# A gate unit at the start and one behind the attention, four scan groups with rows of their own: one change to a hybrid decoder block

## The chip, the cores and the metric

The kernel runs on one core of a Trainium2 chip. The metric is the time of the device for one execution, in microseconds (us). A core has five engines that run side by side, each with an instruction queue of its own, worked off in order: TensorE (PE) for matrix products, VectorE (DVE), ScalarE (ACT), GpSimd (POOL), and SyncE (SP), which here only starts DMA transfers. ACT can start transfers too.

## The reference

One decoder layer over T = 1024 tokens with D = 1024 channels, in float32. Three mixers work on the same normalised input, and sigmoid gates merge them:

```python
h = rms_norm(x, pre_mix_norm)
z, xbc, dt_raw, sb_qkv, nsa_q, nsa_kv, nsa_gate, merge_gate = split(h @ w_in)
y_ssm = ssm_mixer(z, xbc, dt_raw, ...)        # conv, silu, chunked scan in 4 groups, gate by silu(z), norm
y_sb  = stick_breaking_attention(sb_qkv)      # 4 heads of 128, causal, no softmax
y_nsa = nsa_attention(nsa_q, nsa_kv, nsa_gate, ...)  # compressed, selected and window branches, 8 heads of 64
gm = sigmoid(merge_gate).reshape(b, s, 3, D)
mixed = gm[:, :, 0] * (y_ssm @ w_br_ssm) + gm[:, :, 1] * (y_sb @ w_br_sb) + gm[:, :, 2] * (y_nsa @ w_br_nsa)
x = x + rms_norm(mixed @ w_out, post_mix_norm)
h = rms_norm(x, pre_ffn_norm)
gate, val = split(causal_dwconv(h @ ffn_w_up))
return x + rms_norm((gelu(gate) * val) @ ffn_w_down, post_ffn_norm)
```

The scan of a group goes over eight chunks of 128 tokens:

```python
cb = einsum('tn,sn->ts', c, b);  w = cb * decay * dt
y  = einsum('tsh,shp->thp', w, x) + einsum('tn,hpn->thp', c, state) * exp(acum)
state = state * exp(acum[-1]) + einsum('sh,shp,sn->hpn', to_end, x, b)
```

## The kernel before

Channels lie on the partitions and tokens on the free axis. Each float32 operand is split into a rounded part and a rest (`hi`, `lo`; `whi`, `wlo` for weights), and a product is three matmuls: hi·hi, hi·lo, lo·hi. A weight comes by SP's queue into `wraw`; ACT rounds it (`whi`) and POOL subtracts (`wlo`). The order of each engine's instructions is set by a scheduler from the order of the program, the waits between instructions and a model of their durations, so an edit in one place may move instructions in another.

The stages, in order of time in the profiled execution:

- 0 to about 68 us: the input norm in two halves of 512 tokens (`norm`, `normalise`; L440 scales, L442 takes the rest `h_lo`), and small projections with tokens on the partitions (`token_major`; names `ps_t`, `ps_s`, `thi`, `tlo`). Its queries are copied by `q_out` (L434) and stored to memory `q_d` (L435), 16 stores of 128 KB.
- about 65 to 300 us: the scan's inputs (`ssm_units`). Units are computed in pairs by seven products instead of eight. For this, sums of the operand's blocks are made on DVE (`combos`, L537 to L540) and split again by ACT (L561) and DVE (L562); `weights7` prepares the weights' sums. Results go to memory `s_d`: six rows of 128 channels for each of the four groups q (two of x, then B, C, and two of z).
- about 300 to 820 us: sparse attention. While its small steps wait for each other, PE is given pieces of other work: a `Fill` object hands out matmuls of gate units in threes. A gate unit is one block of 128 of the 3072 merge gate channels: 48 matmuls of 128 x 512, a sigmoid in three ACT instructions for each half (L243 to L245, `gate_e`) and two stores to `g_d`. Units 0 to 11 are the fill here (`N_GATES`).
- about 825 to 1171 us: stick-breaking attention, head by head (`sb_stage`). The fill is the next head's projection and gate units 12 to 23 (`SB_GATES` tells which units go with which head, `SB_FILL` how many matmuls per step). In `chain`, a step computes scores (`sa`, `sz`), rounds the running sums (`s_hi` on ACT, `s_lo` on POOL), weights (`w_hi`, `w_lo`) and adds the weighted values into `ps_o` or `ps_b`. Head 3 has no next head: its fill is gate units 18 to 23. At its start, group 0's six rows are loaded.
- about 1168 to 1292 us: the four scans (`ssd_stage`). Each is a generator: in a slot, `front` of a chunk makes `dec` (ACT), `xd` (DVE), `Bc` (ACT) and `W` (POOL), and `back` adds the chunk's result and carries the state. The last slots gate with z, square, and take the mean over channels (one-column matmuls with `ones`), a norm. `SSD_AT` gives the slot in which each group starts. Rows lie in buffers: group 0 in `row` (one buffer each), group 1 in `third`, group 2 in `row` again, group 3 in `row` when group 0 has ended.
- from 1292 us: the branch projections and the merge, the output projection, and the gated MLP with its convolution. `load_y` brings back the mixers' outputs; the last four of its sixteen pieces (k = 12 to 15) use buffers of the scans.

Of the kernel before, what the change touches and what calls it, by code (L numbers as in the profile page):

```python
# [10 lines left out]
F32 = mybir.dt.float32  # L11
R32 = mybir.dt.float32r
# [7 lines left out]
T = 1024  # L20
# [141 lines left out]

N_GATES = 12
SB_GATES = (12, 14, 16, 18, 24)

NSA_FILL = (2, 0)
NSA_SLOTS = 9
# [1 line left out]
NSA_EARLY = 32  # L171
NSA_LEAD = 0
NSA_SWITCH = (10, 1)
SB_FILL = (2.2, 2.2, 2.2, 1.6)

SSD_AT = (0, 2, 9, 12)

X_BUFS = 36

# [16 lines left out]
def trunk(ctx: ExitStack, tc: tile.TileContext, A: dict, outT: bass.AP, dbg=None):  # L196
    nc = tc.nc
# [10 lines left out]
    mm, tr = pe(nc.tensor.matmul), pe(nc.tensor.transpose)  # L208
# [33 lines left out]
    def sigmoid(dst, src):  # L242
        act(dst, src, AF.Exp, scale=-1.0)  # L243
        act(dst, dst, AF.Ln, bias=1.0)
        act(dst, dst, AF.Exp, scale=-1.0)  # L245
# [6 lines left out]
    def scratch(name, shape):  # L252
        scr[name] = dram.tile(shape, F32, name=name, tag=name)
        return scr[name]

    y_d = scratch("y_d", [16 * 128, T])
    g_d = scratch("g_d", [24 * 128, T])
# [38 lines left out]
    def hs(h):  # L296
        return slice(h * 512, (h + 1) * 512)
# [13 lines left out]
    hx = ExitStack()  # L311
# [37 lines left out]
    start = ExitStack()  # L349
# [27 lines left out]
    q_d = scratch("q_d", [2, 8, 128, 256])  # L377
# [4 lines left out]
    xs, tm0 = [[], []], []  # L382
# [49 lines left out]
    def q_out(ci, t, ps, scale):  # L432
        q = tmw.tile([128, 256], F32, name="q_out", bufs=2)
        act(q, ps[:, :256], AF.Copy, scale=scale)  # L434
        nc.sync.dma_start(q_d[ci, t], q)  # L435

    def normalise(h, r):
        for k in range(8):
# [5 lines left out]
    for h, tiles in ((0, [[ps_s, ps_s, ps_t, ps_t]]), (1, [[ps_o, ps_d], [ps_s, ps_s]])):  # L444
        *pss, ss = first_half(h, tiles)
        rq, r = norm(h, ss)
# [15 lines left out]
    U_CMP, U_SB, U_SSM, U_GATE = 0, 2, 14, 38  # L462
# [77 lines left out]
        eng.tensor_tensor(b21, b11, b21, op=OP.add)  # L540


    s_d = scratch("s_d", [24 * 128, T])

    def ssm_units():


        wx = early.enter_context(tc.tile_pool(name="wx0", side="right", reuse_waits="tile", bufs=2))
        ev = early.enter_context(tc.tile_pool(name="ev", side="right", reuse_waits="tile", bufs=2))
        rhs = {q: [None] * 4 for q in range(1, 8)}  # L550
        for k in range(4):
            b = [xs[h][k + n] for n in (0, 4) for h in range(2)]
            combos(*b, V)
            for q, n, h in ((1, 0, 0), (2, 4, 0), (3, 4, 1)):
                rhs[q][k] = h_rhs(k + n, h)
            for q, t in zip((6, 5, 4, 7), b):
                rhs[q][k] = t
        for q in (6, 7, 5, 4):
            for k in range(4):
                t, hi, lo = rhs[q][k], x_t(), x_t()  # L560
                act(hi, t, AF.Copy)  # L561
                V.tensor_tensor(lo, t, fl(hi), op=OP.subtract)  # L562
                rhs[q][k] = hi, lo

        def snap(ps):
            t = x_t(F32)
            act(t, ps, AF.Copy)  # L567
            return t

        for q, m in itertools.product(range(4), (0, 2, 1)):  # L570
            u0 = 6 * q + 2 * m
            halos = [ev.tile([128, 4], F32, name="halo", bufs=4) for _ in range(2)]

            def evict(n, h, ps):
                o = ev.tile([128, 512], F32, name="o")
                if m < 2:
                    cu = q * 4 + 2 * m + n
                    conv(o, h, ps, [pvc(PV_CW, 4 * cu + 3 - d) for d in range(4)], pvc(PV_CB, cu), halos[n])
                act(o, o if m < 2 else ps, AF.Silu)
                nc.sync.dma_start(s_d[(u0 + n) * 128:(u0 + n + 1) * 128, hs(h)], o)  # L580

            w = weights7(wx, A["wfm"][U_SSM + u0], A["wfm"][U_SSM + u0 + 1], 512)
            x, y, z, v = ps_d(), ps_s(), ps_t(), (ps_o, ps_b)[m % 2]()
            product(x, w, rhs, 1, True)
            s1 = snap(x)
            product(y, w, rhs, 2, True)
            V.tensor_tensor(y, y, s1, op=OP.add)
            evict(0, 0, y)
            product(x, w, rhs, 6, False)
            s2 = snap(x)  # L590
            product(z, w, rhs, 7, True)
            product(x, w, rhs, 5, False)
            s3 = snap(x)
            product(v, w, rhs, 4, True)
            V.tensor_tensor(s2, z, s2, op=OP.subtract)
            V.tensor_tensor(v, v, s2, op=OP.add)
            evict(1, 0, v)
            V.tensor_tensor(z, z, s3, op=OP.subtract)
            evict(1, 1, z)
            product(x, w, rhs, 3, False)  # L600
            evict(0, 1, x)
# [2 lines left out]
    tc.keep_in_program_order(nc.scalar.preload_act_table_set(TABLE))  # L604
    early.close()


    gp = hx.enter_context(tc.tile_pool(name="gp", reuse_waits="tile", bufs=2))

    def gates(j0, j1, steps=unit_steps):  # L610
        for j in range(j0, j1):
            def evict(h, ps):
                e = gp.tile([128, 512], F32, name="gate_e")
                sigmoid(e, ps)
                nc.sync.dma_start(g_d[j * 128:(j + 1) * 128, hs(h)], e)
            yield from steps(U_GATE + j, evict)

    both = ExitStack()
    keep = both.enter_context(tc.tile_pool(name="keep", side="right", reuse_waits="tile", bufs=1))
    dte = keep.tile([128, 2, 8, 16], F32, name="dte")  # L620
# [19 lines left out]
    def row_t(n, dt=F32):  # L640
        return hd.tile([128, T], dt, name=f"row{n}")

    def ssm_rows(q, row=row_t):
        rows = [row(n) for n in range(6)]
        for n in (0, 1, 2, 3, 4, 5):
            nc.sync.dma_start(rows[n], s_d[(6 * q + n) * 128:(6 * q + n + 1) * 128, :])
        return rows

    ssm = [None] * 4
    sb = ExitStack()  # L650
    sb_stage(nc, tc, sb, locals())
    sb.close()
    hx.close()
    st2 = ExitStack()
    lop = st2.enter_context(tc.tile_pool(name="lo", reuse_waits="tile", bufs=1))
    third = both.enter_context(tc.tile_pool(name="third", side="right", reuse_waits="tile", bufs=1))

    def third_t(n, dt=F32):
        return third.tile([128, T], dt, name=f"third{n}")
# [15 lines left out]
def nsa_stage(nc, tc, es, env):  # L675
    E = L(env)
# [128 lines left out]
    kx_.close()  # L805
    ks_.close()
    E.token_major(3, E.load_tm(3, tmw), ev_values)
    fill = E.Fill(E.gates(0, N_GATES, E.fine_steps))
    fill.take(NSA_EARLY)

    E.sigmoid(sg, dtr[:, :, 16:40])
# [269 lines left out]
def sb_stage(nc, tc, es, env):  # L1081
# [42 lines left out]
    def chain(h, c, ps_z, ps_out, q_hi, q_lo, k_hi, k_lo, v_hi, v_lo):  # L1124
# [52 lines left out]
        def value(kb):  # L1177
            _, c0, _ = cols(kb)
            pz, _, z = st[kb]
            V.tensor_tensor(z[:, c0:], z[:, c0:], pz[:, c0:], op=OP.add)  # L1180
            act(z[:, c0:], z[:, c0:], AF.Exp)
            strict(z, kb)
            w_hi = tl("w_hi", R32)
            w_lo = tl("w_lo", R32)
            act(w_hi[:, c0:], z[:, c0:], AF.Copy)
            (P if SB_WLO else V).tensor_tensor(w_lo[:, c0:], z[:, c0:], fl(w_hi[:, c0:]), op=OP.subtract)
            for n, (l, r) in enumerate(((v_hi, w_hi), (v_lo, w_hi), (v_hi, w_lo))):
                mm(po[:, c0:], l[:, kb, :], r[:, c0:], start=kb == top and n == 0, stop=kb == 0 and n == 2,
                   skip_group_check=True)

        for n in range(top + 3):
# [8 lines left out]
    def attend(h, fill, *qkv):  # L1200
        gens = [chain(h, 1, ps_s, ps_o, *qkv), chain(h, 0, ps_t, ps_b, *qkv)]
        n = m = 0
        while gens:
# [7 lines left out]
                m -= int(m)  # L1211
            n += 1

    st = [[] for _ in range(4)]
    E.Fill(project(0, st[0])).rest()
    cut = SB_GATES
    for h in range(4):
        more = [project(h + 1, st[h + 1])] if h < 3 else []
        if h == 3:
            E.ssm[0] = E.ssm_rows(0)  # L1220
        fill = E.Fill(*more, E.gates(cut[h], cut[h + 1], E.fine_steps))
        attend(h, fill, *st[h])
        fill.rest()


def ssd_stage(nc, tc, es, env):
# [1 line left out]
    A, act, V, P, mm, tr, fl = E.A, E.act, E.V, E.P, E.mm, E.tr, E.fl  # L1228
    ident, ps_s, ps_t, ps_o, ps_b, pvc = E.ident, E.ps_s, E.ps_t, E.ps_o, E.ps_b, E.pvc
    wk = es.enter_context(tc.tile_pool(name="ssd_w", reuse_waits="tile", bufs=2))  # L1230
    def scan(q, x0, x1, B, C, z0, z1):

        xs, zs = (x0, x1), (z0, z1)
        state = wk.tile([128, 4, 64], F32, name="state")

        ac = E.hd.tile([128, 512], R32, name="half")[:16]
# [59 lines left out]
        for c in range(8):  # L1296
            new = front(c + 1) if c < 7 else None
            back(*st)
            yield
            st = new  # L1300

        for n in range(2):
            V.tensor_tensor(xs[n], xs[n], zs[n], op=OP.mult)
# [17 lines left out]
            r0 = (2 * q + n) * 128  # L1321
            nc.sync.dma_start(E.y_d[r0:r0 + 128, :], xs[n])

    st = E.ssm
    gens = [None] * 4
    st[1] = E.ssm_rows(1, E.third_t)
    st[2] = E.ssm_rows(2)
    for n in range(SSD_AT[-1] + 12):
        for q, at in enumerate(SSD_AT):
            if n >= at:  # L1330
                if n == at:
                    gens[q] = scan(q, *st[q])
                if next(gens[q], 0) == 0 and q == 0 and not st[3]:
                    st[3] = E.ssm_rows(3)


def tail_stage(nc, tc, es, env):
# [20 lines left out]
    def load_y(k):  # L1358

        if k >= 12:  # L1360

            n = 2 * (k - 12)
            whole = [E.third_t(n + m, R32) if k < 15 else E.bt0.tile([128, T], R32, name=f"y{m}", bufs=1)
                     for m in range(2)]
        elif k < 8:
            whole = [yq.tile([128, T], R32, name=n) for n in ("yhi", "ylo")]
        else:
            whole = None
        parts = [[x[:, hs(h)] for x in whole] if whole else [hi_t(), hi_t()] for h in range(2)]
        for h in range(2) if not whole else (slice(None),):  # L1370
            hi, lo = parts[h] if not whole else whole
            src = E.y_d[k * 128:(k + 1) * 128, :]
            nc.sync.dma_start(fl(lo), src if whole else src[:, hs(h)])
            act(hi, fl(lo), AF.Copy)
            V.tensor_tensor(lo, fl(lo), fl(hi), op=OP.subtract)
        return parts
# [328 lines left out]
```

## Time and profile before

| | |
|---|---|
| median of 3 runs | 2298.09 us (2297.56 to 2304.38) |
| profiled execution | 2305.39 us, of which the span of instructions is 2303.4 us |
| mean granted TensorE clock | 0.983 |
| busy share of the span | PE 96%, DVE 59%, ACT 50%, POOL 50% |
| moved by DMA | 222.03 MB, mean 96 GB/s |

PE is the engine that matrix products run on; PEld is its weight load, which overlaps with the products. A row of the timeline has start and duration in us, engine, line, operation, output, inputs and shape; an entry in square brackets is the idle time of the engine before it and what ended that. A row of the windows view has the stretch, its length, then busy time and number of instructions of PE, PEld, DVE, ACT and POOL, the granted TensorE clock as a share of the full one, the busy share of the DMA engines, and GB/s. SPq and ACTq are the DMA issues of an engine's queue. Matmuls overlap each other, so the time of one is seen in the distance between starts and not in its duration.

### The profile page before, as it was taken

The page shows a single profiled execution, that of the slowest core. Times are in us where ns is not written, and L with a number is a line of the kernel's source. Part 1 is how long each engine was busy: PE and PEld are TensorE (multiplying, and loading weights), DVE is VectorE, ACT ScalarE, POOL GpSimd, SP SyncE. Part 2 cuts the span into 40 slices and gives each one's busy share as a digit, 9 for nine tenths or more (in the row PEclk, how much of TensorE's full clock was granted, in tenths as well). Part 3 has the DMA queues.
Part 4 walks back from the last instruction along what each step waited for, and adds up shares of the span by engine and source line. Part 5 has one row for each costly group of instructions (what it writes and reads, how often), then busy time and mean ns, then how long its engine had stood idle before and what let it go on. Part 6 is the DMA issues. An engine that isn't in the chain of part 4 may idle for free.

```text
span 2303.4 us, 30001 instructions
## 1 busy us (share of the span) xinstructions
PE 2207.2 (96%) x10807; PEld 1782.1 (77%) x10807; DVE 1349.9 (59%) x2380; ACT 1157.4 (50%) x2165; POOL 1149.0 (50%) x825
## 2 busy tenths in 40 slices
PE   8899999998998999999999999999899999999997
PEld 8778889766675688878867788887678888878886
DVE  8765553367558326656646552349977777753346
ACT  6554433566666746667754331245545555553224
POOL 4676631156645723333333346446578888822213
PEclk9999999999999999999998999999999999999998
DMA  4223332321220011112253164335322222264312
GB/s 168 95 99 104 119 115 74 104 64 35 69 69 10 26 60 42 60 64 96 89 193 120 47 219 137 109 127 175 107 92 83 83 83 83 83 222 132 95 32 74
DMA packets 114196, 222.03 MB, mean 96 GB/s; under 512 B 28032, under 2 KB 42304, under 8 KB 114048
## 3 DMA queue, kind: packets, MB, share of 16 engines
q1 hardware_dynamic: 113760, 219.90, 28.8%
q8 instruction: 85, 1.39, 0.2%
q14 instruction: 63, 0.52, 0.1%
q10 hardware_dynamic: 288, 0.22, 0.0%
HBM read 162.80 MB, written 57.28 MB: 96 GB/s over the span
## 4 chain that ended last, share of the span: by engine, by line
PE 78%; DVE 11%; ACT 3%; issue 3%; DMA 2%; POOL 2%; SPq 0%; DVEq 0%; ACTq 0%; POOLq 0%
PE dense L204 54%; PE ps_s L204 7%; PE ps_o L204 6%; PE ps_t L204 6%; PE ps_b L204 4%; DVE mx L932 1%; POOL wlo L269 1%; DVE u L306 1%; DVE x L1466 1%; DVE osq L1439 1%; DMA wraw<-in_wdn 0%; DVE x L1659 0%; DVE x L1571 0%; POOL lo L1404 0%; DVE o L308 0%
## 5 line engine op out<-in xcount | busy, mean ns | idle before, releaser
L269 POOL TENSOR_TENSOR wlo<-wraw,whi 128x1024 fp32r<-128x1024 f32 (+2 forms) x134 | 265.9, 1984 | 426.3 <-ACT whi L268 412.2
L204 PE MATMUL dense<-hi,whi 128*128 128x512 f32 x816 | 307.3, 391 | 3.6 <-ACT whi L268 3.6
L204 PE MATMUL dense<-hi,wlo 128*128 128x512 f32 x752 | 288.5, 393 | 7.7 <-POOL wlo L269 7.1
L204 PE MATMUL dense<-lo,whi 128*128 128x512 f32 x688 | 268.5, 390 | 0.7 <-POOL lo L1479 0.5
L204 PE MATMUL dense<-h_hi,whi 128*128 128x512 f32 x656 | 264.0, 402 | 2.3 <-ACT whi L507 2.3
L204 PE MATMUL dense<-h_hi,wlo 128*128 128x512 f32 x656 | 256.8, 391 | 0.0
L204 PE MATMUL dense<-h_lo,whi 128*128 128x512 f32 x656 | 256.7, 391 | 0.0
L268 ACT ACTIVATE whi<-wraw 128x1024 fp32r<-128x1024 f32 (+2 forms) x134 | 116.0, 866 | 270.7 <-PE dense L204 230.3
L971 POOL TENSOR_TENSOR wT_lo<-wT,wT_hi 128x512 fp32r<-128x512 f32 x132 | 168.6, 1285 | 98.1 <-ACT wT_hi L970 85.9
L204 PEld LDWEIGHTS dense<-hi,whi 128*128 128x128 f32 x816 | 153.6, 188 | 38.1 <-ACT whi L268 5.7
L204 PE MATMUL dense<-x,uhi 128*128 128x512 f32 x552 | 176.8, 391 | 4.0 <-ACT x L567 2.4
L204 PEld LDWEIGHTS dense<-hi,wlo 128*128 128x128 f32 x752 | 141.6, 188 | 40.4 <-POOL wlo L269 10.1
L204 PEld LDWEIGHTS dense<-lo,whi 128*128 128x128 f32 x688 | 129.6, 188 | 29.1 <-POOL lo L1479 1.4
L204 PEld LDWEIGHTS dense<-h_hi,whi 128*128 128x128 f32 x656 | 123.7, 189 | 27.0 <-ACT whi L507 2.6
L204 PEld LDWEIGHTS dense<-h_hi,wlo 128*128 128x128 f32 x656 | 123.1, 188 | 26.3
L204 PEld LDWEIGHTS dense<-h_lo,whi 128*128 128x128 f32 x656 | 123.7, 189 | 22.2
L1172 POOL TENSOR_TENSOR s_lo<-sa,s_hi 128x512 fp32r<-128x512 f32 (+2 forms) x48 | 53.5, 1115 | 154.0 <-ACT s_hi L1171 151.1
L204 PEld LDWEIGHTS dense<-x,uhi 128*128 128x128 f32 x552 | 103.2, 188 | 27.5 <-ACT x L567 3.7
L960 ACT ACTIVATE wT<-ps_s 128x512 f32<-128x512 f32 x132 | 78.2, 594 | 69.1 <-PE ps_s L204 66.6
L932 DVE TENSOR_REDUCE mx<-ps_t 128x1 f32<-128x384 f32 (+3 forms) x192 | 94.2, 517 | 30.5 <-PE ps_t L204 27.9
L306 DVE SCALAR_TENSOR_TENSOR u<-dense,pv,u 128x510 f32<-128x510 f32 (+1 forms) x140 | 101.9, 737 | 6.4 <-ACT u L302 6.3
L517 POOL TENSOR_TENSOR ulo<-uf,uhi 128x1024 fp32r<-128x1024 f32 x30 | 72.5, 2417 | 60.8 <-ACT uhi L516 60.8
(514 smaller groups left out, 5686.6 us busy)
## 6 DMA issues: line engine op xcount, KB each, us to landing
wraw<-in_wfm SPq DMA_DIRECT2D x62, 512.0 KB, 3.4
wraw<-in_wup SPq DMA_DIRECT2D x52, 512.0 KB, 3.4
s_d<-o SPq DMA_DIRECT2D x48, 256.0 KB, 2.0
g_d<-gate_e SPq DMA_DIRECT2D x48, 256.0 KB, 2.1
ge<-g_d SPq DMA_DIRECT2D x24, 512.0 KB, 3.8
m_d<-u SPq DMA_DIRECT2D x44, 256.0 KB, 2.0
row<-s_d SPq DMA_DIRECT2D x18, 512.0 KB, 4.3
u<-m_d SPq DMA_DIRECT2D x36, 256.0 KB, 4.0
```

The costliest lines, as they stand in the source:

```text
L204: i = f(*a, **k)
L268: act(hi, raw, AF.Copy)
L269: (V if tiles else P).tensor_tensor(lo, raw, fl(hi), op=OP.subtract)
L306: V.scalar_tensor_tensor(o[:, d:], ps[:, :512 - d], taps[d], o[:, d:], op0=OP.mult, op1=OP.add)
L517: P.tensor_tensor(l24, f24, fl(h24), op=OP.subtract)
L932: V.tensor_reduce(mx[:, h, a, n:n + 1], pm[:, :w], axis=AX, op=OP.max)
L960: act(w.rearrange("p h q -> p (h q)"), pz, AF.Exp)
L971: P.tensor_tensor(lo, wf, fl(hi), op=OP.subtract)
L1172: (P if SB_SLO else V).tensor_tensor(s_lo[:, c0:], a[:, c0:], fl(s_hi[:, c0:]), op=OP.subtract)
L1439: eng.tensor_tensor(sums[0], sums[0], sq, op=OP.add)
L1466: e.tensor_tensor(o[j], o[j], x, op=OP.add)
```

## The change

Five edits:

- The query stores are issued by ACT's queue instead of SP's.
- Gate unit 0 is computed between the combos' splits and the first weights of `ssm_units` (`START_GATES`), and the sparse attention's fill has units 1 to 11.
- The last head's fill has units 18 to 22, at two matmuls per step instead of 1.6. Unit 23 is issued after the attention's last matmul.
- `third` has two buffers of each name. Groups 1 and 3 hold x, B and C in them, group 2 in `row`. Rows are loaded by `ssm_rows` for the numbers that it is given; the z rows of groups 2 and 3 are loaded when groups 0 and 1 end. The scans start in slots 0, 3, 8 and 11 instead of 0, 2, 9 and 12.
- In the tail, pieces 12 and 13 of the mixers' outputs go to `row` buffers, 14 and 15 to `third`.

```diff
+START_GATES = 1
 N_GATES = 12
-SB_GATES = (12, 14, 16, 18, 24)
+SB_GATES = (12, 14, 16, 18, 23, 24)
...
-SB_FILL = (2.2, 2.2, 2.2, 1.6)
-
-SSD_AT = (0, 2, 9, 12)
+SB_FILL = (2.2, 2.2, 2.2, 2)
+
+SSD_AT = (0, 3, 8, 11)
...
         act(q, ps[:, :256], AF.Copy, scale=scale)
-        nc.sync.dma_start(q_d[ci, t], q)
+        nc.scalar.dma_start(q_d[ci, t], q)
...
+    gp = hx.enter_context(tc.tile_pool(name="gp", reuse_waits="tile", bufs=2))
+
+    def gates(j0, j1, steps=unit_steps):
...
                 V.tensor_tensor(lo, t, fl(hi), op=OP.subtract)
                 rhs[q][k] = hi, lo
+
+        Fill(gates(0, START_GATES)).rest()
...
-    def ssm_rows(q, row=row_t):
-        rows = [row(n) for n in range(6)]
-        for n in (0, 1, 2, 3, 4, 5):
-            nc.sync.dma_start(rows[n], s_d[(6 * q + n) * 128:(6 * q + n + 1) * 128, :])
-        return rows
-
-    ssm = [None] * 4
+    def ssm_rows(q, ns, row=row_t):
+
+        for n in ns:
+            r = row(n)
+            nc.sync.dma_start(r, s_d[(6 * q + n) * 128:(6 * q + n + 1) * 128, :])
+            ssm[q].append(r)
+
+    ssm = [[] for _ in range(4)]
...
-    third = both.enter_context(tc.tile_pool(name="third", side="right", reuse_waits="tile", bufs=1))
+    third = both.enter_context(tc.tile_pool(name="third", side="right", reuse_waits="tile", bufs=2))
...
-    fill = E.Fill(E.gates(0, N_GATES, E.fine_steps))
+    fill = E.Fill(E.gates(START_GATES, N_GATES, E.fine_steps))
...
-                mm(po[:, c0:], l[:, kb, :], r[:, c0:], start=kb == top and n == 0, stop=kb == 0 and n == 2,
+                last[0] = mm(po[:, c0:], l[:, kb, :], r[:, c0:], start=kb == top and n == 0, stop=kb == 0 and n == 2,
...
-            E.ssm[0] = E.ssm_rows(0)
+            E.ssm_rows(0, range(6))
...
+    with tc.issue_after(last[0].ins):
+        E.Fill(E.gates(cut[4], cut[5], E.fine_steps)).rest()
...
-    def scan(q, x0, x1, B, C, z0, z1):
-
-        xs, zs = (x0, x1), (z0, z1)
+    def scan(q, x0, x1, B, C):
+
+        xs = x0, x1
...
+        z0, z1 = zs = held[q][4:]
...
-    st[1] = E.ssm_rows(1, E.third_t)
-    st[2] = E.ssm_rows(2)
+    for q, ns, row in ((1, range(4), E.third_t), (2, range(4), E.row_t), (1, (4, 5), E.row_t), (3, range(4), E.third_t)):
+        E.ssm_rows(q, ns, row)
...
-                    gens[q] = scan(q, *st[q])
-                if next(gens[q], 0) == 0 and q == 0 and not st[3]:
-                    st[3] = E.ssm_rows(3)
+                    gens[q] = scan(q, *held[q][:4])
+                if next(gens[q], 0) == 0 and q < 2 and len(held[q + 2]) < 6:
+                    E.ssm_rows(q + 2, (4, 5))
...
-            n = 2 * (k - 12)
-            whole = [E.third_t(n + m, R32) if k < 15 else E.bt0.tile([128, T], R32, name=f"y{m}", bufs=1)
-                     for m in range(2)]
+            whole = [(E.third_t, E.row_t)[k < 14](2 * (k % 2) + m, R32) for m in range(2)]
```

More of the change, by code (lines that the diff above doesn't have):

```diff
@@ L540, in combos, with evict @@
         eng.tensor_tensor(b21, b11, b21, op=OP.add)
+    gp = hx.enter_context(tc.tile_pool(name="gp", reuse_waits="tile", bufs=2))
+    def gates(j0, j1, steps=unit_steps):
+        for j in range(j0, j1):
+            def evict(h, ps):
+                e = gp.tile([128, 512], F32, name="gate_e")
+                sigmoid(e, ps)
+                nc.sync.dma_start(g_d[j * 128:(j + 1) * 128, hs(h)], e)
+            yield from steps(U_GATE + j, evict)
     s_d = scratch("s_d", [24 * 128, T])
@@ L605, in trunk @@
     early.close()
[L608 to L616, printed above, removed]
     both = ExitStack()
@@ L1212, in attend @@
             n += 1
+    last = [None]
     st = [[] for _ in range(4)]
@@ L1322, in scan @@
             nc.sync.dma_start(E.y_d[r0:r0 + 128, :], xs[n])
-    st = E.ssm
+    held = E.ssm
     gens = [None] * 4
-    st[1] = E.ssm_rows(1, E.third_t)
-    st[2] = E.ssm_rows(2)
+    for q, ns, row in ((1, range(4), E.third_t), (2, range(4), E.row_t), (1, (4, 5), E.row_t), (3, range(4), E.third_t)):
+        E.ssm_rows(q, ns, row)
     for n in range(SSD_AT[-1] + 12):
```

## The prediction

> **What bounds it now.** I read the page's busy times and its chain first, then the windows by stage, then the timelines at the four places that the diff touches.
>
> ```profile
> PE 2207.2 (96%) x10807; PEld 1782.1 (77%) x10807; DVE 1349.9 (59%) x2380; ACT 1157.4 (50%) x2165; POOL 1149.0 (50%) x825
> PE 78%; DVE 11%; ACT 3%; issue 3%; DMA 2%; POOL 2%; SPq 0%; DVEq 0%; ACTq 0%; POOLq 0%
> ```
>
> TensorE (PE) is the bound, and the matmuls are the same in number and kind in both kernels: the change can win only where PE stands idle or runs at a lower clock. The windows tell where (length; busy time of PE, PEld, DVE, ACT, POOL; PE clock; DMA share; GB/s):
>
> ```profile
> 68.00:82.00 14.00, 7.41 (x19) 5.12 (x19) 13.58 (x16) 6.97 (x13) 11.95 (x4) 0.76 0.25 84
> 790.00:850.00 60.00, 60.00 (x277) 47.77 (x276) 6.45 (x22) 27.37 (x52) 23.88 (x16) 1.00 0.20 64
> 986.00:1160.00 174.00, 174.00 (x802) 144.81 (x801) 98.90 (x169) 120.85 (x238) 56.61 (x38) 1.00 0.26 90
> 1171.00:1292.00 121.00, 113.81 (x720) 83.58 (x720) 71.95 (x161) 56.33 (x168) 55.64 (x53) 0.90 0.35 123
> 1182.00:1193.00 11.00, 7.90 (x35) 5.56 (x36) 4.20 (x8) 3.64 (x13) 4.37 (x4) 0.69 0.96 388
> 1227.00:1262.00 35.00, 33.55 (x186) 26.98 (x186) 20.68 (x46) 13.86 (x32) 5.87 (x7) 0.76 0.43 151
> 1262.00:1292.00 30.00, 29.81 (x212) 21.75 (x211) 20.30 (x48) 15.38 (x51) 20.12 (x19) 1.00 0.06 19
> ```
>
> PE is idle for half of 68–82 (operand preparation). It is saturated at 790–850 (end of the sparse attention) and at 986–1160 (stick-breaking attention). In the scans, 1171–1292, it looks busy, but 720 small matmuls in 121 us at clock 0.90 are a slow queue, not a full one.
>
> **The gate unit, the currency of the change.**
>
> ```profile
> 1157.27 0.39 PE L204 MATMUL dense<-h_lo,whi 128*128 128x512 f32 x1
> 1164.53 0.39 PE L204 MATMUL ps_s<-s_hi,rtab 128*128 128x512 f32 x1
> 825.47 20.88 PE dense L204 x92
> L243 ACT ACTIVATE gate_e<-dense x48: 575/582/601, 385.8 to 1168.8; 128x512 f32<-128x512 f32 x48
> ```
>
> Matmuls overlap, so their price is the distance of starts: 32 of them from 1157.27 to 1164.53, 0.227 us each (92 in 20.88 agrees). A unit is 48: 10.9 us where PE is full. Beside it go six sigmoid pieces of some 0.6 us on ACT. Two units move, 21.8 us in all: unit 0 to the start, unit 23 behind the attention's last matmul.
>
> **Sparse attention.** Its fill loses unit 0, whose 48 matmuls come off the saturated stretch: −10.9. Some steps between fill matmuls become bare; I give back 1.2 and take −9.7 (−10.9 to −8.5).
>
> **The start.**
>
> ```profile
> 44.23 24.01 SPq L435 DMA_DIRECT2D q_d<-q_out  x12
> 45.12 5.36 DVE L440 SCALAR_TENSOR_TENSOR x<-x,pv,ps_b 128x512 f32<-128x512 f32 x8 [1.47 <-PE ps_b L204]
> 67.53 13.48 DVE L562 TENSOR_TENSOR x<-x 128x512 fp32r<-128x512 f32 x15
> 71.59 0.50 PE L204 MATMUL ps_o<-x,ahi 128*128 128x512 f32 x1 [3.47 <-ACT x L561]
> 73.29 1.06 ACT L507 ACTIVATE whi<-wraw 128x1024 fp32r<-128x1024 f32 x1 [1.75 <-DMA wraw<-in_wfm]
> 74.39 0.79 PE L204 MATMUL dense<-h_hi,whi 128*128 128x512 f32 x1 [2.30 <-ACT whi L507]
> 24.04 2.83 POOL L508 TENSOR_TENSOR wlo<-wraw,whi 128x1024 fp32r<-128x1024 f32 x1 [23.53 <-ACT rt L237]
> 25.14 2.28 DVE L405 TENSOR_TENSOR ss<-ss,sq 128x512 f32<-128x512 f32 x1 [0.46 <-DVE rv L236]
> 27.52 0.69 DVE L405 TENSOR_TENSOR ss<-ss,sq 128x512 f32<-128x512 f32 x1
> 1.25 0.45 ACTq L381 DMA_DIRECT2D tab<-in_c_tab  x1
> ```
>
> Two chains set this stage. SP's queue is held from 44 to 68 by 12 query stores, so a weight load comes late: ACT waits 1.75 us for it, PE 2.30. The other is DVE, which from 45 to 81 has no break: while it splits operands, PE gets 19 matmuls in 14 us. Stores on ScalarE free the first chain; 16 issues of some 0.45 us (ACTq at 1.25) go on ACT, which is busy for half of 68–82, so I cost them at nothing (without that cover: 16 × 0.45 = 7). The second chain stays, and the order of the changed program lengthens it. Ahead of the second half's scale transposes, which release DVE's part at 45.12, stand nineteen gate matmuls where twelve of the first combo product stood, and two token-major ones more: 7 × 0.227 + 0.2, some +2. The gate's wlo runs on POOL beside the one already there, and while one runs (24.04 for 2.83), DVE's 0.69 us add took 2.28: +2. In 68–82 PE loses 6.6 us idle and 7.41 × 0.24 = 1.8 by the clock: 8.4 of the gate's 10.9 us would be hidden with the chain unmoved. But the stage ends when the chain does, 4 later, and I add 1 for matmuls that then still queue: **+5** (+2 if the earlier load gives the 2.3 back and little queues, +8 if DVE's shift and a third of the gate are exposed).
>
> [...]
>
> **End of the stick-breaking attention.** Unit 23 leaves the saturated stretch: −10.9. But it was the cover of the last steps.
>
> ```profile
> 1155.00 0.69 DVE L1153 TENSOR_SCALAR sa<-ps_s 128x512 f32<-128x512 f32 x1 [2.52 <-PE ps_s L204]
> 1160.19 1.30 POOL L1172 TENSOR_TENSOR s_lo<-sa,s_hi 128x512 fp32r<-128x512 f32 x1 [4.42 <-ACT s_hi L1171]
> 1166.32 0.69 DVE L1180 TENSOR_TENSOR sz<-sz,ps_s 128x512 f32<-128x512 f32 x1 [4.16 <-PE ps_s L204]
> 1167.04 0.63 ACT L1181 ACTIVATE sz<-sz 128x512 f32<-128x512 f32 x1 [3.78 <-DVE sz L1180]
> 1168.27 0.61 ACT L1185 ACTIVATE w_hi<-sz 128x512 fp32r<-128x512 f32 x1
> 1169.82 0.68 DVE L1186 TENSOR_TENSOR w_lo<-sz,w_hi 128x512 fp32r<-128x512 f32 x1
> 1170.77 0.39 PE L204 MATMUL ps_o<-w_lo,row 128*128 128x512 f32 x1
> ```
>
> From the last score to the last value matmul eleven pieces follow one another: ten of 0.6 to 0.7 us and s_lo's 1.30, 7.9 us of work, and about 10 with the hand-overs between engines. In the changed order about 18 small attention matmuls (18 × 0.23 = 4.1 us) stand there and no gate matmul, since those are held until the last one. PE then idles 10.2 − 4.1 ≈ 6 to 7: **+7** (+4 if the hand-overs cost nothing, +10 if the chain is nearly as stretched as before, 1155.0 to 1170.8, less the 4.1).
>
> **The scans.** Before, from the last value matmul (1171.1) to the first matmul of the tail's sparse branch (1291.59) are 120.5 us; behind that matmul PE's order is the same in both.
>
> ```profile
> 1167.81 0.49 PE L204 MATMUL ps_s<-half,sel 16*128 16x512 f32 x1
> 1262.78 0.66 PE L204 MATMUL ps_o<-W,xd 128*64 128x128 f32 x8
> 1289.50 0.66 PE L204 MATMUL dense<-W,xd 128*64 128x128 f32 x8 [0.16 <-DVE row L1291]
> 1291.59 0.71 PE L204 MATMUL ps_o<-third,whi 128*128 128x512 f32 x2
> L204 PE MATMUL ps_o<-W,xd x128: 272/273/476, 1173.1 to 1288.4; 128*64 128x128 f32 x128
> L204 PE MATMUL dense<-W,xd x104: 272/273/477, 1191.6 to 1289.9; 128*64 128x128 f32 x104
> 1174.45 5.41 SPq L646 DMA_DIRECT2D third<-s_d  x6
> PE ps_t L204 <- DMA third<-s_d: 2.6, 3, 1.0
> 1245.05 4.43 PE L204 MATMUL dense<-ones,third 128*128 128x1 f32 x30 [0.56 <-ACT third L1304]
> ```
>
> A chunk's second half ("back") has 8 W,xd matmuls: (128 + 104) / 8 = 29 backs lie in that stretch. When two scans run and no norm stands between, as from 1262.78 to 1291.59, there are 10 backs: 2.9 us each. From 1227 to 1262, with both norm chains (16 one-column matmuls each, such as 1245.05) and the clock at 0.76, only 4 backs come; 35 − 4 × 2.9 = 23 us are the norms' price. At 1182–1193 the second scan's loads, queued on SP at 1174.45 behind other stores, cost 2.6 us of waits and a clock of 0.69.
>
> After: gate unit 23 runs first, and the first back follows after its 10.9 us plus the 5.3 from first front matmul to first back (1167.81 to 1173.1), 16.2. Twenty-nine backs at 2.9 are 84. The third-buffer loads land under the gate unit, so their wait goes. With starts at slots 0, 3, 8, 11 the norms of groups 0 and 1 meet two running scans instead of about one; I take half their price, 12 (6 to 20). 16.2 + 84 + 12 = 112, against 120.5: **−8.5** (−14 to −2, the backs at 2.7 to 3.1). Note what is not there: no engine waits for the fourth group's loads before, so the buffers alone remove only the 2.6.
>
> Freed at nothing: the gate stores' issue, and the tail's last four y loads, which go to other buffers and are needed 9 us or more after their tiles come free.
>
> **Sum.** +5 − 9.7 − 10.9 + 7 − 8.5 = −17. The profiled execution took 2305.39 us (span 2303.4); that gives 2288. The median of the runs is 2298.09, 7.3 lower, so 2281.
>
> **Rivals.**
> 1. No change. The scans keep their own mean rate, norms included: (1291.6 − 1173.1) / 29 = 4.09 us a back. Then 16.2 + 118.5 = 134.7, +14 instead of −8.5, and the sum is +6: 2304. For it: the trace shows no wait that the new buffers remove beyond 2.6 us. Against it: 2.9 us a back wherever two scans run free.
> 2. Slower. With group 2 starting at slot 8 and group 3 at 11, three scans stand around the norms of groups 0 and 1 in PE's fixed order, and each norm holds all of them: the price of 23 us grows by half (+12) on top of rival 1, or 4.5 us a back: 16.2 + 130 = 147, sum +18: 2316. It decides from 136 us for the stretch (120.5 + 8.6 that the other terms win + 7).
> 3. The start isn't hidden: DVE's chain shifts by the gate's whole 10.9. The sum is −11: 2287, still faster.
> 4. The clock. At 68–82, after idle times of 3.47 and 2.30 us, the clock is 0.76. If the bare 7 us ahead of unit 23 do the same to its first half, it costs some 2 to 3 us more: 2284. [...]
>
> **How the numbers follow.** 0.3% is 7 us, also the spread of the three runs, and about what a measurement of this kernel can tell. The forecast with its near variants (3, 4 and the terms' bounds): 0.62; rival 1: 0.18; rival 2: 0.20. The forecast's own terms reach from 2268 to 2295; to leave out no more than 2 in 10 the range goes to rival 1's 2304. Of rival 1 a third falls on the faster or the slower side: faster 0.65, same 0.14, slower 0.21.
>
> **What would show it.** Right: PE's idle time at the operand preparation gone, with the first combo product at some 75 us; the sparse attention about 5 us earlier at its end than before; a bare 6 to 7 us before the last value matmul; the tail's first sparse-branch matmul 112 us behind it. Wrong: norms with no backs between them, a stretch over 130 us, ACT's query stores holding the operand split, or a first product later than 80.

## The result, and the profile after

The changed kernel takes 2311.92 us (median of 7 runs, 2308.16 to 2315.94); the kernel before 2301.05 us in the runs beside it. The ratio is 1.0047, 95% interval 1.0030 to 1.0064: slower by some 11 us, where 17 us faster were forecast. The profiled execution is 2311.68 us, its span 2310.0.

Every execution also lists its mean granted TensorE clock, and this explains most of the spread between runs of one kernel: of the 19 runs of the kernel before beside e1 to e4, the fastest, 2294.29, has 0.987, the slowest, 2307.34, has 0.981. So the table splits each mean time into time × (1 − clock), what a lower clock can have taken, and the rest; the two add up to the mean, not to the median. It is an accounting (idle time at a low clock costs nothing), averaged over runs because a clock is listed to 0.001, and it doesn't say in which stage the clock was low. The row of before is its series beside e9 to e12; the means of its three series are 2301.1, 2300.8 and 2300.6. The last column is from the one profiled execution of each kernel: the stretch of the scans, from the end of the attention's last value matmul to the first matmul of the tail's sparse branch.

| kernel | runs | median us | mean clock | time × (1 − clock) | rest | scans, traced |
|---|---|---|---|---|---|---|
| before | 30 | 2300.1 | 0.9850 | 34.6 | 2266.0 | 120.4 |
| after | 7 | 2311.9 | 0.9813 | 43.3 | 2268.6 | 133.7 |
| e1 unit 23 in the head | 12 | 2304.5 | 0.9831 | 39.0 | 2265.7 | 123.3 |
| e2 no unit at the start | 5 | 2315.8 | 0.9798 | 46.8 | 2268.4 | 133.7 |
| e3 old slots | 6 | 2313.8 | 0.9810 | 44.0 | 2269.3 | 136.7 |
| e4 scans' part alone | 8 | 2307.5 | 0.9816 | 42.4 | 2265.4 | 122.5 |
| e5 before, 64 columns | 11 | 2298.4 | 0.9874 | 29.0 | 2269.3 | 121.5 |
| e6 = e1, 64 columns | 6 | 2292.1 | 0.9878 | 27.9 | 2265.4 | 118.4 |
| e7 after, 64 columns | 12 | 2299.7 | 0.9864 | 31.3 | 2269.5 | 125.9 |
| e8 unit 23 behind, alone | 5 | 2313.5 | 0.9796 | 47.2 | 2266.4 | 133.6 |
| e9 after without unit 23 | 12 | 2302.2 | 0.9802 | 45.6 | 2255.3 | 123.4 |
| e10 = e6, old slots | 12 | 2304.7 | 0.9862 | 31.9 | 2272.0 | 127.1 |
| e11 = e6, stores on SP | 12 | 2297.5 | 0.9870 | 29.9 | 2265.9 | 118.3 |
| e12 = e6, split gating | 7 | 2291.4 | 0.9891 | 24.9 | 2266.1 | 113.3 |

From before to after, 8.7 of the 11 us are in the clock's column. The page and the windows of the changed kernel:

```profile
PE 2213.3 (96%) x10807; PEld 1784.7 (77%) x10807; DVE 1346.9 (58%) x2380; ACT 1156.0 (50%) x2165; POOL 1145.7 (50%) x825
PE 80%; DVE 10%; ACT 4%; issue 3%; DMA 1%; POOL 1%; SPq 0%; DVEq 0%; ACTq 0%; POOLq 0%
```

```profile
68.00:82.00 14.00, 14.00 (x71) 11.79 (x69) 12.48 (x21) 10.81 (x23) 7.32 (x3) 1.00 0.23 76
794.00:854.00 60.00, 57.15 (x266) 44.92 (x265) 10.47 (x32) 27.56 (x62) 21.50 (x16) 1.00 0.17 55
982.00:1152.00 170.00, 170.00 (x789) 141.72 (x788) 93.24 (x165) 118.64 (x235) 56.04 (x38) 1.00 0.24 83
1152.00:1164.00 12.00, 7.83 (x19) 4.36 (x18) 4.83 (x7) 5.43 (x10) 1.40 (x2) 0.65 0.61 220
1164.00:1299.00 135.00, 129.60 (x771) 95.56 (x771) 72.35 (x163) 61.10 (x179) 55.67 (x54) 0.89 0.31 112
1226.00:1244.00 18.00, 17.45 (x76) 13.68 (x76) 7.22 (x20) 3.10 (x6) 3.54 (x4) 0.53 0.10 30
1262.70:1271.90 9.20, 9.20 (x55) 7.37 (x52) 2.37 (x9) 2.10 (x6) 2.84 (x4) 0.63 0.17 57
```

The hole at 68–82 is closed. A new one stands at 1152–1164, at the end of the attention, with the clock at 0.65. In the scans PE is busy nearly always, but at 0.53 and 0.63 around the two norms. The timeline at the places of the change:

```profile
1151.04 0.39 PE L205 MATMUL ps_t<-row,row 128*128 128x128 f32 x2
1157.11 0.79 PE L205 MATMUL ps_s<-half,sel 16*128 16x512 f32 x1 [3.82 <-DVE sz L1184]
1163.26 0.63 PE L205 MATMUL ps_o<-w_lo,row 128*128 128x512 f32 x1
1175.53 1.29 DVE L1266 TENSOR_TENSOR xd<-ps_t,dte 128x512 f32<-128x512 f32 x2 [12.62 <-PE dense L205]
1177.73 0.50 PE L205 MATMUL ps_s<-half,sel 16*128 16x512 f32 x1 [2.01 <-ACT dec L1258]
1182.52 0.79 PE L205 MATMUL ps_o<-W,xd 128*64 128x128 f32 x8
1227.70 5.27 PE L205 MATMUL ps_b<-ones,row 128*128 128x1 f32 x24
1262.74 5.17 PE L205 MATMUL dense<-ones,row 128*128 128x1 f32 x32
1297.57 0.70 PE L205 MATMUL ps_o<-row,whi 128*128 128x512 f32 x2
```

Gate unit 23 runs from 1163.69. The first scan instruction on DVE (`xd`) reads transposes that were done soon after 1151 (`ps_t`), but it starts at 1175.53, when the unit's last matmul is over; DVE idles 12.62 us before it. The first back comes at 1182.52, 18.6 us after the attention. From the attention's end to the tail's sparse branch are 1297.57 − 1163.9 = 133.7 us, against 120.4 before. Twenty-four one-column matmuls take 5.27 us, 0.22 each; at full clock they are 0.11 apart (30 in 3.40 us in the kernel before, shown at the end).

### The profile page after: what moved, and what is told of

It is laid out like the page before. It is cut to its first block, busy times and chain, and to the rows that moved or that the text cites. A ratio compares the mean times of both kernels' runs of the same rounds, so it can differ in the third digit from the quotient of the medians.

```text
span 2310.0 us, 30003 instructions
## 1 busy us (share of the span) xinstructions
PE 2213.3 (96%) x10807; PEld 1784.7 (77%) x10807; DVE 1346.9 (58%) x2380; ACT 1156.0 (50%) x2165; POOL 1145.7 (50%) x825
## 4 chain that ended last, share of the span: by engine, by line
PE 80%; DVE 10%; ACT 4%; issue 3%; DMA 1%; POOL 1%; SPq 0%; DVEq 0%; ACTq 0%; POOLq 0%
PE dense L205 56%; PE ps_s L205 7%; PE ps_o L205 7%; PE ps_t L205 6%; PE ps_b L205 4%; DVE mx L936 1%; POOL wlo L270 1%; DVE x L1473 1%; DVE u L307 1%; DVE x L1578 1%; DVE osq L1446 1%; DMA wraw<-in_wdn 0%; DVE x L1666 0%; ACT h_hi L399 0%; DVE o L309 0%
## 5 line engine op out<-in xcount | busy, mean ns | idle before, releaser
L205 PEld LDWEIGHTS dense<-hi,wlo 128*128 128x128 f32 x752 | 142.4, 189 | 41.6 <-POOL wlo L270 10.4
L205 PEld LDWEIGHTS dense<-h_hi,wlo 128*128 128x128 f32 x656 | 123.4, 188 | 26.5
```

The lines of the kernel that those rows point to most:

```text
L205: i = f(*a, **k)
```

## The experiments

All were timed beside the kernel before. The theories: A, the loss is gate unit 23 behind the attention; B, it is the scans' part with its new slots; C, it is the start; later N, the norms' one-column matmuls lower the clock, against G, the gaps do.

**e1, unit 23 back in the last head.**

```diff
-SB_GATES = (12, 14, 16, 18, 23, 24)
+SB_GATES = (12, 14, 16, 18, 24, 24)
-SB_FILL = (2.2, 2.2, 2.2, 2)
+SB_FILL = (2.2, 2.2, 2.2, 1.6)
```

> The changed kernel with gate unit 23 back in the last head's fill (fill 1.6 per step). Theory A (the unit behind the attention is the loss: it runs with nothing beside it, its cover of the attention's last steps is gone, and the first scan chunk comes late): the stretch from the last value matmul to the tail's sparse branch returns from 133 us to about 120, the bare steps before the last value matmul vanish, and the time is about 2298 (14 below the changed kernel's 2312, a little under before's 2301). Theory B (the new start slots, with three scans around the two norms, are the loss): the stretch stays over 130 us less the unit's 11, and the time stays within 3 us of 2312.

2304.51, ratio to before 1.0014 (1.0004 to 1.0025). Seven us come back, half of what A said: A is part of it, not all.

**e2, no unit at the start** (`START_GATES = 0`).

> The changed kernel with gate unit 0 back in the sparse attention's fill. From the two traces the start costs 4.0 us up to the sparse attention and the fill without the unit wins 7.7 back: theory A and B both expect about 3.6 more than the changed kernel, 2315.5. Rival C (the start is the loss, for instance by what it does to the loads): about 2302.

2315.78, 1.0057 (1.0045 to 1.0069): 3.9 slower than the changed kernel, as the traces said. The start gate is a gain; C falls.

**e3, the old slots** (`SSD_AT = (0, 2, 9, 12)`).

> The changed kernel with the scans' starts in slots 0, 2, 9, 12 as before; buffers and gate units as changed. Theory B: the norms meet fewer scans, the stretch falls from 133 to about 123, the time to about 2302. Theory A: within 3 us of 2312.

2313.84, 1.0049 (1.0037 to 1.0061): within 2 us. With unit 23 behind the attention the slots decide nothing.

**e4, the scans' part alone.** The kernel before with the scans' part of the change: the buffers of `third`, the new load order and slots, the tail's four loads.

> The kernel before with only the scans' part of the change (third with two buffers, the new load order, slots 0, 3, 8, 11, the tail's four loads). Theory A: the second scan's wait for its loads (2.6 us) goes or shrinks and nothing else, about 2298 to 2301. Theory B: 8 to 12 us slower than before, about 2310.

2307.49, 1.0029 (1.0018 to 1.0041): 6 to 7 us slower, so B holds too, for the part as a whole. In the windows, the stretch of its two norms and below it that of before:

```profile
1218.00:1270.00 52.00, 47.68 (x260) 39.42 (x261) 27.81 (x63) 18.10 (x44) 13.08 (x14) 0.70 0.21 72
```

```profile
1220.00:1262.00 42.00, 39.27 (x234) 31.49 (x234) 27.41 (x56) 16.59 (x39) 10.02 (x10) 0.80 0.40 138
```

52 × 0.30 = 15.6 us go to the clock, against 42 × 0.20 = 8.4, and in the table its rest is not longer than before's. That led to N. But the two windows differ in length, and the whole stretch of the scans is only 2.1 us longer than before (122.5 against 120.4): the waits for the second scan's loads are gone, and two new waits of 3.3 and 3.2 us for a state's copy on DVE stand around the norms. So these two traces place some 2 of the 7 us in the scans; where the rest arises they don't show.

**e5, e6, e7, 64 columns instead of one** in the norms' matmuls, in the kernel before, in e1 and in the changed kernel. The extra columns are copies.

```diff
-            mm(ps[:, m:m + 1], zs[n][:, m * 128:(m + 1) * 128], E.ones[:, 0:1], start=n == 0, stop=n == 1)
+            mm(ps[:, m * 64:(m + 1) * 64], zs[n][:, m * 128:(m + 1) * 128], E.ones[:, 0:64], start=n == 0, stop=n == 1)
-        E.rsqrt_mean(rt, v, ps[:, 0:8], 256)
+        E.rsqrt_mean(rt, v, ps[:, 0:512:64], 256)
```

> The kernel before, in which each of the norms' one-column matmuls (32 in a group) computes 64 equal columns instead of one; nothing else. Theory N (a run of one-column matmuls counts as an idle TensorE: the clock is halved 2 to 3 us after it begins and stays so for 7 to 10 us): the half-clock stretches at 1230 and 1247 (17 us in all, 8.5 us lost) and those of the last two norms go or shrink; the wider matmuls cost 1 to 5 us; time 2293 to 2298 against 2301. Theory G (the clock falls for the gaps between instructions, or the time is the loads of weights): the stretches stay, 2301 to 2306.

2298.43, 0.9991 (0.9982 to 0.9999): just faster than before, just outside what N said. 5.6 us less in the clock's column, 3.3 more in the rest.

> The kernel with gate unit 23 in the last head's fill (2304.5 before) and 64 columns in the norms' matmuls. Theory N: the two norms' 27 us at half clock shrink to under 10, 2293 to 2299. Theory G: 2304 to 2309.

2292.05, 0.9967 (0.9952 to 0.9981): 12.5 us below e1, and faster than before. Not all of it can be put down to the norms: in the two profiled executions the attention ends at 1172.47 (e1) and 1164.51 (e6), 8 us apart ahead of everything that was edited, and the scans' stretch is 4.9 us shorter (123.3 to 118.4).

> The changed kernel with 64 columns in the norms' matmuls. Theory N: the stretches at 1227 and 1265 (24 us at half clock, 12 lost) shrink; the one behind the bare end of the attention at 1156 stays; 2301 to 2306 against 2312. Theory G: 2312 to 2317.

2299.65, 0.9998 (0.9982 to 1.0013): 12.3 us below the changed kernel, level with before. The stretch of the scans in the changed kernel, and below it in e7:

```profile
1163.89:1297.57 133.68, 128.28 (x767) 94.47 (x765) 70.92 (x162) 61.05 (x178) 55.49 (x54) 0.89 0.32 113
1169.85:1295.77 125.92, 120.50 (x766) 89.10 (x765) 71.16 (x162) 60.90 (x178) 55.18 (x54) 0.95 0.33 120
```

It is 7.8 us shorter; in the 60 us behind it, where the last two norms stand, the clock goes from 0.94 to 1.00, which is 3.6 us more. So N holds in all three, though the times lie outside what it forecast in each. But G is not empty. The windows of before and, below, two of e5:

```profile
1290.00:1350.00 60.00, 60.00 (x309) 49.52 (x306) 28.18 (x55) 14.77 (x26) 11.52 (x11) 0.91 0.39 129
```

```profile
1235.00:1249.00 14.00, 13.96 (x62) 11.57 (x63) 5.83 (x13) 3.54 (x11) 3.25 (x3) 0.51 0.43 150
1290.00:1350.00 60.00, 60.00 (x324) 49.47 (x323) 29.47 (x57) 17.08 (x30) 11.57 (x10) 1.00 0.50 159
```

At the last two norms (1290–1350), where PE doesn't wait, the clock is full with the wider matmuls and 0.91 without. At 1235, where PE had waited 1.77 us, it is halved all the same (0.51 in 1235–1249), with no one-column matmul in the norm: there it was a wait that the half clock followed.

**e8, unit 23 behind the attention, alone**: of the change only the lines on `SB_GATES`, `SB_FILL`, `last` and `issue_after`.

> The kernel before with gate unit 23 behind the attention's last matmul and a fill of 2 per step, and nothing else of the change. The two parts being independent, as runs so far make it (the changed kernel less the one with the unit in the head: 7.4 us): 2301 + 6 to 9, 2307 to 2310, with some 10 us at half clock behind the bare steps of the attention's end. If the unit costs only because the scans' order was changed with it: 2301 within 3.

2313.54, 1.0056 (1.0042 to 1.0070): 12.5 us above before, more than expected, nearly all in the clock's column (47.2 against 34.6). Its timeline has the same two holes as the changed kernel's:

```profile
1160.21 0.50 PE L204 MATMUL ps_s<-half,sel 16*128 16x512 f32 x1 [3.82 <-DVE sz L1180]
1180.61 0.50 PE L204 MATMUL ps_s<-half,sel 16*128 16x512 f32 x1 [2.01 <-ACT dec L1254]
```

So the parts one by one: this unit 13, the scans 7 (e4), the start's unit −4 (e2), and the stores −2 to −5 (e11 below, measured beside the start's unit): 11 to 14 together, against 11 for the whole. That they add up so well is in part luck: each is uncertain by some 3 us, and taken out of the changed kernel the same unit is worth 7.4 (e1), not 13.

**e9, the changed kernel without unit 23's matmuls**; its rows get unit 22's values.

```diff
+                if j == 22:
+                    nc.sync.dma_start(g_d[23 * 128:24 * 128, hs(h)], e)
-SB_GATES = (12, 14, 16, 18, 23, 24)
+SB_GATES = (12, 14, 16, 18, 23, 23)
```

> The changed kernel without the 48 matmuls of gate unit 23 (its rows get unit 22's values), so that the attention's last steps are as bare and nothing stands behind them. If the unit behind the attention covers nothing (theory A): its 10.9 us and the late first chunk go, 2296 to 2301. The kernel with the unit in the head took 2304.5; less the unit's 10.9 that is 2293.6, so what this run takes above 2294 is the price of the bare steps with the half clock behind them: 4 to 8 us expected, 2298 to 2302. If the unit fills waits of the scans' start (rival): less than 8 us below the changed kernel, over 2304.

2302.16, 1.0003 (0.9990 to 1.0015): 9.7 us less than with the unit by the medians, 11.0 by the means, so little or none of its 10.9 us fills anything there. The trace shows what differs:

```profile
1155.01 1.29 DVE L1268 TENSOR_TENSOR xd<-ps_t,dte 128x512 f32<-128x512 f32 x2 [0.69 <-PE ps_t L205]
```

Without the unit, `xd` runs as soon as its transposes are done, during the attention's last steps; with it, `xd` waited for the unit's end (1175.53; in e8 1178.41). In the program the buffers that the unit reads from are given back ahead of the scans, and the scans' work buffers are opened behind that; that these share memory would explain the wait, but it was not tried. The bare steps with the clock behind them cost, by estimate, 2302.2 − (2304.5 − 10.9) = 8.6 us, a little over the upper end expected. That is their price in e9, where some 17 us run at half clock, against 10.2 in the changed kernel.

**e10, e11, e12**, each one edit on e6: the old slots; the query stores back on SP's queue; the gating ahead of a norm in four pieces.

```diff
         for n in range(2):
-            V.tensor_tensor(xs[n], xs[n], zs[n], op=OP.mult)
-            act(zs[n], xs[n], AF.Square)
+            for h in range(4):
+                s = slice(256 * h, 256 * h + 256)
+                V.tensor_tensor(xs[n][:, s], xs[n][:, s], zs[n][:, s], op=OP.mult)
+                act(zs[n][:, s], xs[n][:, s], AF.Square)
```

> The kernel with gate unit 23 in the head's fill and 64 columns (2292), with the scans' starts in slots 0, 2, 9, 12. If the clock was what hid a gain of the new slots: 2296 to 2300. If the slots are worth nothing by themselves, as they were in the changed kernel: 2292 within 3.

2304.67, 1.0015 (1.0004 to 1.0026): 12.6 us above e6, more than expected, by the means 6.6 of it in the rest and 4.0 in the clock's column. Once unit 23 and the norms' clock are out of the way, the new slots are a gain; e3 had hidden it. But most of it is a gain over the old slots with the new buffers and load order, whose stretch is 127.1 us; the kernel before's slots with their own load order and 64 columns take 121.5 (e5), only 3.1 more than e6. Its waits are spread, the largest:

```profile
PE ps_o L205 <- DVE rv L237: 2.4, 1, 2.4
PE ps_t L205 <- DMA third<-s_d: 1.9, 2, 1.0
PE ps_s L205 <- DVE row L1328: 1.8, 1, 1.8
```

Which of them the slots remove, one by one, was not tried.

> The same kernel (2292) with the query stores back on SP's queue. If the queue was what made the first weights late, as predicted: 2 to 3 us slower, 2294 to 2295. If the load waits for ACT's reading of an earlier weight instead (it was issued at 74.4 in the changed kernel, later than the 69.9 of before): 2292 within 1.5.

2297.52, 0.9979 (0.9967 to 0.9992): 5 us above e6 by the medians but 2.4 by the means, since the runs lie wide (2288.22 to 2301.48). SP's queue in its timeline, and below it in e6's:

```profile
59.01 17.23 SPq L436 DMA_DIRECT2D q_d<-q_out  x7
77.75 6.59 SPq L503 DMA_DIRECT2D wraw<-in_wfm  x2
```

```profile
74.39 6.57 SPq L503 DMA_DIRECT2D wraw<-in_wfm  x2
```

The stores hold the weight's load for 3.4 us.

> The same kernel (2292) with the multiplication by z and the square ahead of each norm in four pieces of 256 tokens, so that they run as chunks end and a state's copy doesn't queue behind two of 1.6 us on DVE. If the half clock at 1214 and 1245 (20 us in all) begins with PE's waits of 3.2 and 1.3 us for that copy: the waits go and most of the half clock too, 2280 to 2287. If other waits take their place: 2289 to 2293.

2291.45, 0.9962 (0.9946 to 0.9978): the lowest median, but not apart from e6's. PE's longest wait in the scans of e6, and the stretch behind it there and in e12:

```profile
PE ps_b L205 <- DVE state L1285: 3.2, 1, 3.2
```

```profile
1213.00:1228.00 15.00, 14.43 (x66) 12.86 (x66) 4.93 (x17) 2.86 (x6) 1.89 (x2) 0.54 0.11 36
```

```profile
1213.00:1228.00 15.00, 13.60 (x113) 10.74 (x111) 11.62 (x29) 6.29 (x19) 4.87 (x6) 1.00 0.22 73
```

The 3.2 us wait for a state's copy is gone, and with it the halved stretch: 66 matmuls in 15 us become 113. The scans' stretch is 5.1 us shorter (113.3 against 118.4). In the medians little of it is left; why, stays open.

## Why the prediction was wrong, point by point

**The bound and the currency** were right: PE is the bound, and a unit is 10.9 us where it is full (e9: 9.7 to 11.0 gone with the unit).

**The start, +5:** the size was right. In the traces the first scan input is 6.6 us later, the end of that stage 4.3, the sparse attention's first value matmul 4.0. DVE's two chains ran as the prediction had them: POOL's two subtractions in a row (2.78 and 2.82 us), one add of 2.29 us and one tiny operation of 2.33 beside them, where the same add took 0.68 without them (29.46). That the stores held the weights was right in kind (e11), though the load came no earlier in the changed kernel (74.39), since its whole stage is later. The first combo product came at 80.55, past the 80 that the prediction named as a sign of being wrong: PE's hole was filled, but that sign was set too tight, for the stage's end still moved by only 4.3.

**The sparse attention, −9.7:** −7.7 in the traces. The stretch at its end isn't full any more (57.15 of 60), so more became bare than the 1.2 given back. Start and fill together won 3.6, and e2 measured 3.9.

**The end of the stick-breaking attention, −10.9 + 7:** −3.6 in the profiled execution, so the sum was right there, in part by luck. PE idles only 4.2 us there (12.00 − 7.83 in 1152–1164), not 6 to 7; what fills up the term is the clock, which is halved for 10.2 us from within the hole on. Some 8 of these fall on the attention's last steps, the last 2 on gate matmuls.

**The scans, −8.5:** this is the step that failed; +13.3 in the traces. From the first back on, the stretch took 118.4 us before, 96 were forecast, and 115.1 were measured. Three terms of 112 us were mis-sized. The first back: 16.2 forecast, 18.6 measured, +2.4. The backs: 29 × 2.9 = 84 was forecast, but in the free stretch from 1182.52 to 1226 there are 14 in 43.5 us, 3.1 each, +6. The norms, the largest: "I take half their price, 12"; what remains of 133.7 − 18.6 − 29 × 3.1 is 25, their whole price as before (23), +13. The choice of half was argued from scans that run beside a norm, but this price is only in part waiting. Of the 64 one-column matmuls, 56 take 10.4 us (5.27 + 5.17, and 0.22 apart once the clock is low), and what other scans run beside the norm slows too: eight matmuls of `W` and `xd` take 1.12 us at 1240.13, at half clock, against 0.66 at 1221.99, so that more scans beside it made it no cheaper here. Some 8 of the 25 us are shown to be the clock behind the one-column matmuls: with 64 columns and nothing else changed the stretch is 7.8 us shorter (e7). How the other 17 divide into the matmuls themselves and into waits was not separated. The kernel before's 0.76 in 1227–1262 showed the clock's part, and the prediction quoted that row and called it the norms' price without asking what set the clock.

**The rivals.** Rival 1 (the scans keep their mean rate) was nearly right: it gave 134.7 us for the stretch, which was 133.7, and +6 for the sum, and the two profiled executions differ by 6.3. That the median is 2312 and not its 2304 comes from the base (below). Rival 2 said that norms would hold three scans and gave 147 us; its mechanism wasn't seen. Rival 4 put the half clock on the first half of unit 23, at 2 to 3 us; it fell on the bare steps ahead of the unit instead, and only 2 us of it, 1 us lost, on the unit. In pieces of 0.2 us, the windows view of the changed kernel from 1140 to 1350 shows 1.00 or 0.50, and a value between them only in the piece in which it goes from one to the other: half clock for 3.4 us behind the wait that ends at 1177.73, and for 10.2 us from 1155.5, within the hole.

**The profile's own time.** The step from 2305.39 to the median was a shift of the same kernel's clock: that execution had 0.983, the mean of 30 is 0.985. The two profiled executions differ by 6.3 us, the medians by 11. The terms account for the 6.3 (+4.0 − 7.7 − 3.6 + 13.3 = 6.0); the other 5 us come from the base, since the profiled execution of the kernel before took 4.8 us more than the mean of its runs, and that of the changed kernel as long as the mean.

## What to carry to other kernels

Read the granted clock beside PE's busy share, stage by stage: here PE was "busy" at 0.53 in a stretch with one-column matmuls (changed kernel, 1226–1244) and at 0.54 in one behind a wait of 3.2 us (e6, 1213–1228), and with more scans beside the norms their price was 25 us, against 23 before. Before work that covers a tail is moved behind it, price the tail bare, with the half clock that came with its waits (here 10.2 us with one of 3.82), and look whether the next stage's first instructions on the other engines can run beside the moved work: here they couldn't, and 10.9 us of matmuls moved cost some 8.6 us in front and 10 behind. And try a part again once another loss is off: the slots that were worth at most 2 us in the changed kernel were worth 12 us in e6, against the old slots with the same load order.

## What the runs showed of the hardware

A run of one-column matmuls, back to back and 0.11 us apart at full clock, was followed by a halved TensorE clock though no gap was over 0.6 us (kernel before, from 1245.05; the clock in 1241–1247 is 1.00, in 1247–1254 0.53):

```profile
1241.00:1247.00 6.00, 5.00 (x33) 3.60 (x31) 6.00 (x9) 5.03 (x11) 0.61 (x1) 1.00 0.34 113
1247.00:1254.00 7.00, 7.00 (x36) 6.02 (x37) 2.44 (x9) 2.19 (x5) 2.53 (x2) 0.53 0.78 280
```

It was so even where PE had no gap at all, at the kernel before's last norm:

```profile
1328.91 3.40 PE L204 MATMUL dense<-ones,row 128*128 128x1 f32 x30
1326.00:1329.00 3.00, 3.00 (x17) 2.46 (x15) 0.69 (x1) 0.07 (x1) 0.00 (x0) 1.00 0.55 179
1329.00:1336.00 7.00, 7.00 (x41) 6.24 (x40) 1.36 (x5) 2.41 (x5) 1.27 (x1) 0.77 0.53 160
```

With 64 columns of the same operands the clock stayed full where PE had no wait (e5, 1.00 in 1290–1350, against 0.91 in the kernel before). What it is in a one-column run that the half clock follows, for instance that it counts as idle time, as N had it, the runs don't show.

Half clock also came with waits of PE, partly with shorter waits behind them. In the rows of e5 to e9 its length is an estimate, 2 × (1 − clock) × the window's length, as if the clock there too were only 1.00 or 0.50:

| kernel | wait, us, and its end | half clock |
|---|---|---|
| changed | 3.82, 1157.11 | 10.2 us from 1155.5 |
| changed | 2.01, 1177.73 | 3.4 us from 1179.4 |
| e5 | 1.77, 1235.03 | 0.51 in 1235–1249, 13.7 us |
| e6 | 3.19, 1213.58 | 0.54 in 1213–1228, 13.8 us |
| e8 | 3.82, 1160.21 | 0.75 in 1155–1168, 6.5 us |
| e9 | 2.86, 1161.35 | 0.67 in 1155–1181, 17.2 us |

In e5's 1220–1235, where PE was idle for 2.9 us, the last 1.77 of them the wait above, the clock was 1.00. And the time of one kernel follows its mean clock from run to run: in the 19 runs of the kernel before beside e1 to e4, 13 us between 0.987 and 0.981, which is 0.006 of the time.
